# Transposing the middle values of an FFN by the DMA crossbar in two 16-bit planes

## The chip, the cores and the metric

The kernel runs on one core of one Trainium2 chip. The metric is device time in microseconds (us) of one execution.

## The reference

Two decoder layers run over one sequence of 512 positions with 1024 channels, all in float32. The first layer mixes with a recurrent block, the second with a chunked spatial gate. Around each mixer stand two feed-forward networks (FFN), four in all:

```python
def swiglu(x, w_in, w_out):
    g, u = jnp.split(x @ w_in, 2, axis=-1)
    return (jax.nn.silu(g) * u) @ w_out

for i in range(DEPTH):                       # DEPTH = 2
    h = h + 0.5 * swiglu(rms_norm(h, ffn1_norm[i]), ffn1_w_in[i], ffn1_w_out[i])
    hn = rms_norm(h, mix_norm[i])
    h = h + (recurrent_mixer(hn, ...) if i % 2 == 0 else spatial_gating_mixer(hn, ...))
    h = h + 0.5 * swiglu(rms_norm(h, ffn2_norm[i]), ffn2_w_in[i], ffn2_w_out[i])
return rms_norm(h, final_norm)
```

`w_in` is 1024 x 5632 and `w_out` 2816 x 1024. The middle values, `silu(g) * u`, are 512 x 2816.

## The kernel before

Every large product is computed with three float32r matmuls: each operand is split into a high part (`hi`, `whi`: a ScalarE copy with rounding) and the rest (`lo`, `wlo`: a VectorE subtraction), and hi x hi, lo x hi and hi x lo are added in PSUM (lines 385 to 387). On top of this, large blocks are multiplied by a scheme of seven products instead of eight (`seven`). Its left operands are sums of the four quarters A11, A12, A21, A22 of a block: S1 = A21 - A22 and, out of it, S2, S4 and S3 (`Group.s2`, `s4`, `s3`).

The unit of work is a step, a `Sub`: one weight tile of 128x1024 is loaded by the SP queue (line 135), for some products a second weight block is added by an accumulating DMA of the POOL queue (line 138) or by VectorE (line 87), the tile is split into `whi` and `wlo`, and the step's matmuls follow, mostly 12 of 128x512. All engines get their instructions in the order in which one loop over the steps writes them. In step i the loop splits the weights up to step i + 3 (`SPLIT_AHEAD`), runs what other code has hooked to the phases "pre", "mid" and "rest" of this step, asks for more weight loads, writes the step's matmuls, and runs "end" and "late". There are four buffers for `whi` and `wlo` and eight for raw weights. All other values lie in 60 slots of 128x512 float32 (`sp`).

An FFN is done in three parts (`FF_PARTS`): part 0 has a pair (2 column blocks of 128, `pair_plain`, eight steps) and a chunk of 4 column blocks (`chunk`, 14 steps), parts 1 and 2 have two chunks each. After the blocks of a part, `out_blocks` multiplies its middle values by the rows of `w_out`. In the first FFN, the pair's steps lie within the chunk of part 0.

The middle values come out with tokens on the partitions and are needed with channels on the partitions. `left_blocks` does that: it is called when the values of the first half of the tokens are ready (`half` 0: quarters A11 and A12) and again for the second half (A21 and A22). With `whole`, which the pair and the first chunk of parts 1 and 2 use, nothing is done for half 0, and after half 1 all quarters are transposed in one place: `Group.turn` writes TensorE transposes of 128x128 against an identity (line 267) into PSUM at a step's "end", 16 for a chunk and 8 for a pair. `Group.take` copies A11, A12 and A22 out of PSUM on ScalarE (line 96) and makes S1 from PSUM with one subtraction on VectorE (line 87). `Group.parts` then splits each left operand into hi and lo. The other chunks transpose each half by itself, and the steps below do not touch them.

Of the kernel before, what the change touches and what calls it, by code (L numbers as in the profile page):

```python
# [7 lines left out]

F32 = mybir.dt.float32
F32R = mybir.dt.float32r  # L10
AF = mybir.ActivationFunctionType
ALU = mybir.AluOpType

P = 128
D = 1024
T = 512
# [36 lines left out]
def trunk(ctx: ExitStack, tc: tile.TileContext, a: dict, out: bass.AP):  # L53
    nc = tc.nc
    PS = bass.MemoryType.PSUM
    cp = ctx.enter_context(tc.tile_pool(name="cp", bufs=1))
    sp = ctx.enter_context(tc.tile_pool(name="sp", bufs=SLOTS))
# [9 lines left out]
    def nm(s):  # L67
        uid[0] += 1
        return f"{s}_{uid[0]}"

    def slot(dt=F32, name="s"):
        return sp.tile([P, T], dt, tag="s", name=nm(name))
# [10 lines left out]
    def f32(t):  # L83
        return t.bitcast(F32)

    def tt(o, x, y, op):
        nc.vector.tensor_tensor(out=o, in0=x, in1=y, op=op)  # L87
# [4 lines left out]
    def stt(o, x, s, y, op0, op1):  # L92
        nc.vector.scalar_tensor_tensor(out=o, in0=x, scalar=s, in1=y, op0=op0, op1=op1)

    def act(o, x, f, **k):
        nc.scalar.activation(out=o, in_=x, func=f, **k)  # L96

    def split(src):

        w = src.shape[-1]  # L100
        hi, lo = slot(F32R, "hi")[:, :w], slot(F32R, "lo")[:, :w]
        act(hi, src, AF.Copy)
        tt(lo, src, f32(hi), ALU.subtract)
        return hi, lo
# [46 lines left out]
    class Sub:  # L151
# [19 lines left out]
        def split(self, between=None):  # L171

            if self.hi is not None:
# [4 lines left out]
            _, k, c = src.shape  # L178
            self.hi = wp.tile([P, 1024], F32R, tag="whi", name=nm("whi"))[:, : k * c].rearrange(
                "p (k c) -> p k c", k=k)  # L180
            self.lo = wp.tile([P, 1024], F32R, tag="wlo", name=nm("wlo"))[:, : k * c].rearrange(
                "p (k c) -> p k c", k=k)
            for q in ((slice(0, 1), slice(1, 2)) if self.raw.halves else (slice(0, k),)):
                act(self.hi[:, q, :], src[:, q, :], AF.Copy)
                tt(self.lo[:, q, :], src[:, q, :], f32(self.hi[:, q, :]), ALU.subtract)
# [29 lines left out]
    def hook(n, phase, fn):  # L215


        hooks.setdefault((n, phase), []).append(fn)
# [29 lines left out]
    class Group:  # L248
# [21 lines left out]
        def take(self, name, ps, gains=None):  # L270
# [11 lines left out]
            if gains is None:  # L282
                act(t, ps, AF.Copy)
            else:
                for q, g in zip(qs, gains):
                    act(t[:, q], ps[:, q], AF.Copy, scale=g)

        def direct(self, name, ps, gains):

            hi, lo = self.hl[name] = slot(F32R, "hi")[:, : self.n * H], slot(F32R, "lo")[:, : self.n * H]  # L290
            cs = [(slice(q * H, (q + 1) * H), g) for q, g in enumerate(gains)]
            for c, g in cs:
                act(hi[:, c], ps[:, c], AF.Copy, scale=g)
            for c, g in cs:
                stt(lo[:, c], ps[:, c], g, f32(hi[:, c]), ALU.mult, ALU.subtract)

        def stage(self, n, name, src, gains=None, parts=True, where=None, direct=0, turn=None, lag=0):


            st = {}  # L300
            hook(n if turn is None else turn, "end", lambda: st.update(ps=self.turn(src, where)))
            first = name == "A21"
            hook(n + 1, "pre" if first else "mid", lambda: self.take(name, st["ps"], gains))
            if direct:
                hook(n + direct, "mid", lambda: self.direct(name, st["ps"], gains))
            hook(n + max(direct, 1), "mid", st.clear)
            if parts:
                hook(n + 1 + lag, "mid", lambda: self.parts("S1" if first else name))
# [136 lines left out]
    def xt(t, n):  # L445
        return X[:, t, n * 512 : (n + 1) * 512]

    def square(t, n):
        junk = slot(name="junk")
        act(junk, xt(t, n), AF.Square, accum_out=ss[:, n * TT + t : n * TT + t + 1])  # L450

# [89 lines left out]
    class TileNorm:  # L541
# [29 lines left out]
        def take(self, half):  # L571
            for k in KORDER:
                ps = self.ps[k // 2][:, k % 2 * H : (k % 2 + 1) * H]
                if half == 0:
                    self.z[k] = (slot(F32R, "zh"), slot(F32R, "zl"))
                hi, lo = (t[:, half * H : (half + 1) * H] for t in self.z[k])
# [137 lines left out]
    def left_blocks(g, tiles, half, lag=1, whole=False, where=aux):  # L714


        def src(k, t0):
            return lambda q, s: tiles[t0 + s][:, (k * g.n + q) * P : (k * g.n + q + 1) * P]

        n = now[0] + lag  # L720
        if whole:
            if half == 0:
                return

            where = [bank, bank, None, None] if g.n == 2 else Halves(where).parts + Halves(aux).parts
            for at, name, k, t0, w in zip((n + 1, n + 2, n, n + 1), ("A11", "A12", "A22", "A21"), (0, 1, 1, 0), (0, 0, 2, 2),
                                          where):
                g.stage(at, name, src(k, t0), None, name != "A22", w, turn=n)
        elif half == 0:
            g.stage(n, "A11", src(0, 0))  # L730
            g.stage(n + 1, "A12", src(1, 0), turn=n)
            return
        else:
            g.stage(n, "A22", src(1, 2), None, False)
            g.stage(n + 1, "A21", src(0, 2), turn=n)
        sums(g, n + 3)
# [16 lines left out]
    def sums(g, n, s3=2):  # L753
        for i, fn in zip((0, 1, s3), (g.s2, g.s4, g.s3)):
            hook(n + i, "pre", fn)
# [12 lines left out]
    def chunk(w_in, f0, nt, group, opening=None, whole=False):  # L768
# [25 lines left out]
        def p3(s, ps):  # L794
            tt(c2[s], ps, c2[s], ALU.subtract)
            stt(c2[s], c2[s], rt(s), c1[s], ALU.mult, ALU.mult)
            ht[s] = c2[s]
            if s == 1:
                left_blocks(group, ht, 0, 2 if opening else 1, whole=whole)
# [5 lines left out]
        def q4(s, ps):  # L805
            s4 = slot(name="s4")[:, :w]
            act(s4, ps, AF.Silu, scale=rt(2 + s))
            stt(c5[s], c5[s], rt(2 + s), s4, ALU.mult, ALU.mult)
            ht[2 + s] = c5[s]
            if s == 1:  # L810
                left_blocks(group, ht, 1, whole=whole)
# [4 lines left out]
    def pair_plain(w_in, f0, group, first=False):  # L816
# [26 lines left out]
        def post(half):  # L843
            for s in range(2):
                ps, t = st[half, s], 2 * half + s
                if t not in ht:
                    silu(half, s)
                o = slot(name="h")[:, :w]
                stt(o, ps[:, w:], S.rt[:, t : t + 1], ht[t], ALU.mult, ALU.mult)
                ht[t] = o  # L850
            left_blocks(group, ht, half, 2, True, bank if first else aux)
# [52 lines left out]
    class FinalNorm:  # L904
# [86 lines left out]
        def keep(self, scale):  # L991
# [3 lines left out]
            def parts():  # L995
                self.x = split(xt(1, 1))
                self.eye = cp.tile([P, P], F32R, tag="eye", name="eye")
                act(self.eye, ident, AF.Copy, scale=1.0 / scale)
# [637 lines left out]
```

## Time and profile before

| | us |
|---|---|
| median of 3 runs | 1607.85 |
| range of the runs | 1607.69 to 1607.88 |
| span of the profiled execution, first to last instruction | 1607.4 |
| median less that span | 0.45 |
| TensorE matmul busy | 1598.5 (99%) |
| TensorE weight load busy | 1330.9 (83%) |
| VectorE busy | 1367.5 (85%) |
| ScalarE busy | 1037.4 (65%) |
| GpSimd busy | 222.6 (14%) |

All rows of the profile are from the one profiled execution. In a group's row stand the source line, engine, operation, written and read tiles, shape and count, then the busy time in us and the mean duration of one in ns, and the engine's idle time before it with what ended most of it. PE is TensorE's matmuls, PEld its weight loads, DVE VectorE, ACT ScalarE, POOL GpSimd, SPq the SP queue. In a row of the timeline stand start and duration in us; a bracket tells how long the engine had been idle and what released it.

### The profile page before, as it was taken

What the parts mean: (1) busy time and instruction counts of PE and PEld (TensorE: products, weight loads), DVE (VectorE), ACT (ScalarE), POOL (GpSimd) and SP (SyncE); (2) the same over time, 40 slices, a digit from 0 to 9 for tenths busy, and PEclk for the clock granted to TensorE, in tenths of its full rate; (3) what the DMA queues carried; (4) which work ended last, traced back from release to release, by engine and by line L of the source; (5) the groups of instructions that cost most, each with busy time, mean ns of one, the idle gap of its engine ahead of it and who ended that gap; (6) DMA issues with size and microseconds to landing.
All of it is one profiled execution on the core that took longest, in us unless ns stands there. A gap on an engine that the chain in (4) does not pass through costs nothing.

```text
span 1607.4 us, 20846 instructions
## 1 busy us (share of the span) xinstructions
PE 1598.5 (99%) x7453; PEld 1330.9 (83%) x7453; DVE 1367.5 (85%) x1834; ACT 1037.4 (65%) x1507; POOL 222.6 (14%) x201
## 2 busy tenths in 40 slices
PE   9999999999999999999999999999999999999998
PEld 7888888898888888888888888888888888888886
DVE  6998888888998787878987978878978988879778
ACT  7656556658777556656776565566886765565566
POOL 2111111100011111111101111111211011111110
PEclk9999999999999999999999999999999999999999
DMA  8877876944383786877837768768887557686793
GB/s 286 190 163 166 214 183 152 221 125 112 88 215 84 189 210 153 213 164 163 203 98 180 173 161 217 182 152 209 225 190 189 157 128 187 171 210 160 166 214 89
DMA packets 164264, 279.31 MB, mean 174 GB/s; under 512 B 11472, under 2 KB 37184, under 8 KB 164160
## 3 DMA queue, kind: packets, MB, share of 16 engines
q1 hardware_dynamic: 114656, 184.84, 36.7%
q0 software_dynamic: 47712, 91.30, 33.9%
q10 hardware_dynamic: 1792, 1.84, 0.4%
q8 instruction: 59, 0.97, 0.2%
q14 instruction: 45, 0.37, 0.1%
HBM read 275.84 MB, written 2.10 MB: 173 GB/s over the span
## 4 chain that ended last, share of the span: by engine, by line
PE 99%; DVE 0%; ACT 0%; issue 0%
PE A L386 14%; PE A L387 14%; PE A L385 14%; PE C L386 8%; PE C L387 8%; PE C L385 8%; PE p L834 5%; PE B L386 4%; PE B L385 4%; PE B L387 4%; PE e L267 4%; PE r L225 2%; PE r L226 2%; PE r L227 2%; PE Q L386 1%; PE Q L385 1%
## 5 line engine op out<-in xcount | busy, mean ns | idle before, releaser
L87 DVE TENSOR_TENSOR wlo<-raw,whi 128x1024 fp32r<-128x1024 f32 (+1 forms) x537 | 637.5, 1189 | 182.9 <-ACT whi L96 178.0
L96 ACT ACTIVATE whi<-raw 128x1024 fp32r<-128x1024 f32 (+1 forms) x537 | 554.9, 1034 | 368.5 <-PE A L386 116.4
L385 PE MATMUL A<-whi,hi 128*128 128x512 f32 x1016 | 399.3, 393 | 0.0
L387 PE MATMUL A<-wlo,hi 128*128 128x512 f32 x1016 | 395.9, 390 | 0.0
L386 PE MATMUL A<-whi,lo 128*128 128x512 f32 x1016 | 395.7, 389 | 0.0
L387 PEld LDWEIGHTS A<-wlo,hi 128*128 128x128 f32 x1016 | 190.7, 188 | 40.1 <-DVE wlo L87 0.4
L386 PEld LDWEIGHTS A<-whi,lo 128*128 128x128 f32 x1016 | 190.9, 188 | 38.4 <-DVE lo L87 0.3
L385 PEld LDWEIGHTS A<-whi,hi 128*128 128x128 f32 x1016 | 190.8, 188 | 38.2
L385 PE MATMUL C<-whi,hi 128*128 128x512 f32 x560 | 218.3, 390 | 0.0
L386 PE MATMUL C<-whi,lo 128*128 128x512 f32 x560 | 218.0, 389 | 0.0
L387 PE MATMUL C<-wlo,hi 128*128 128x512 f32 x560 | 218.0, 389 | 0.0
L138 POOL DMA_DIRECT2D raw<-in_ffn_w_in_dram x82 | 99.1, 1216 | 733.5 <-DVE raw L87 374.3
L138 POOL DMA_DIRECT2D raw<-in_ffn_w_out_dram x72 | 83.4, 1208 | 367.4 <-DVE wlo L87 181.9
L87 DVE TENSOR_TENSOR raw<-raw,raw 128x1024 f32<-128x1024 f32 x108 | 129.3, 1197 | 0.5
L96 ACT ACTIVATE hi<-a 128x512 fp32r<-128x512 f32 (+1 forms) x188 | 112.0, 601 | 19.1 <-DVE a L87 16.2
L87 DVE TENSOR_TENSOR lo<-a,hi 128x512 fp32r<-128x512 f32 (+1 forms) x188 | 122.0, 655 | 2.2 <-ACT hi L96 2.1
L386 PEld LDWEIGHTS C<-whi,lo 128*128 128x128 f32 x560 | 105.1, 188 | 22.4 <-DVE lo L87 0.7
L385 PEld LDWEIGHTS C<-whi,hi 128*128 128x128 f32 x560 | 105.1, 188 | 21.8
L387 PEld LDWEIGHTS C<-wlo,hi 128*128 128x128 f32 x560 | 105.1, 188 | 21.7
L96 ACT ACTIVATE c<-A 128x512 f32<-128x512 f32 x132 | 77.7, 597 | 70.3 <-PE A L387 70.3
L385 PE MATMUL B<-whi,hi 128*128 128x512 f32 x280 | 109.3, 390 | 0.0
L386 PE MATMUL B<-whi,lo 128*128 128x512 f32 x280 | 109.1, 389 | 0.0
(180 smaller groups left out, 2090.9 us busy)
## 6 DMA issues: line engine op xcount, KB each, us to landing
raw<-in_ffn_w_in_dram SPq DMA_DIRECT2D x161, 512.0 KB, 4.5
raw<-in_ffn_w_out_dram SPq DMA_DIRECT2D x100, 512.0 KB, 5.5
raw<-in_ffn_w_in_dram POOLq DMA_DIRECT2D x82, 512.0 KB, 7.0
raw<-in_ffn_w_out_dram POOLq DMA_DIRECT2D x60, 512.0 KB, 8.1
raw<-in_sg_w_in_dram SPq DMA_DIRECT2D x20, 512.0 KB, 7.0
raw<-in_ffn_w_in_dram SPq DMA_DIRECT2D x34, 256.0 KB, 5.1
raw<-in_rec_w_in_dram SPq DMA_DIRECT2D x16, 512.0 KB, 3.9
raw<-in_sg_w_in_dram POOLq DMA_DIRECT2D x12, 512.0 KB, 7.9
```

The lines of the kernel that those rows point to most:

```text
L87: nc.vector.tensor_tensor(out=o, in0=x, in1=y, op=op)
L96: nc.scalar.activation(out=o, in_=x, func=f, **k)
L138: nc.gpsimd.dma_start(out=self.v, in_=src, accum_op=ALU.add)
L225: nc.tensor.matmul(ps, wh, xh, start=start, stop=False)
L226: nc.tensor.matmul(ps, wh, xl, start=False, stop=False)
L227: nc.tensor.matmul(ps, wl, xh, start=False, stop=stop)
L267: nc.tensor.transpose(ps[:, o : o + P], src(q, s), ident)
L385: nc.tensor.matmul(ps, zh, wh, start=fresh and i == 0, stop=False, **k)
L386: nc.tensor.matmul(ps, zl, wh, start=False, stop=False, **k)
L387: nc.tensor.matmul(ps, zh, wl, start=False, stop=end, **k)
L834: nc.tensor.matmul(bank_of(half, s), z, (sub.lo if m == 2 else sub.hi)[:, q, :], start=left[2] == "2" and (h, q, m) == (0, 0, 0), stop=lef ...
```

## The change

For the pair and the first chunk of parts 1 and 2, `left_blocks` calls the new `Group.cross` for each half as it becomes ready, in place of TensorE's transposes. At "mid" of step n, ScalarE copies each of the half's two token tiles into two planes: the low and the high 16 bits of each float32, viewed as uint16 (`planes`). At "rest" of the same step, the SP queue issues four transposing DMAs from SBUF to SBUF, two for each of the half's two quarters (`move`). At "mid" of steps n + 3 and n + 4, ScalarE copies the transposed planes of one quarter each back into one float32 tile (`merge`). A21 is merged into the tile of S1, and VectorE subtracts A22 there at step n + 5 (`s1`). The hi and lo parts of A11, A12 and S1 are made from step n + 5 on, and S2, S4 and S3 follow at n + 6 to n + 8 of the second half. The planes and the transposed planes take slots of `sp`. The line numbers of the changed kernel are one larger at the helpers.

```diff
+        def cross(self, n, names, tiles):
+            w, pl, dt = 4 * self.n * P, [], {}
+            def planes():
+                for h in tiles:
+                    t = sp.tile([P, 2 * T], U16, tag="s", name=nm("pl"))[:, :w]
+                    act(t.rearrange("p (k b f) -> p k b f", k=2, b=2),
+                        h.bitcast(U16).rearrange("p (k f b) -> p k b f", k=2, b=2), AF.Copy)
+                    pl.append(t)
+                tiles.clear()
+            def move():
+                for name, k in names:
+                    d = dt[name] = sp.tile([P, 2 * T], U16, tag="s", name=nm("dt"))[:, :w]
+                    v = d.rearrange("p (m s t) -> p m s t", s=2, t=P)
+                    for s, t in enumerate(pl):
+                        nc.sync.dma_start_transpose(out=v[:, :, s, :], in_=t[:, k * w // 2 : (k + 1) * w // 2])
+                pl.clear()
+            def merge(name):
+                t = self.new("S1" if name == "A21" else name)
+                act(t.bitcast(U16).rearrange("p (x b) -> p b x", b=2), dt.pop(name).rearrange("p (b x) -> p b x", b=2), AF.Copy)
+            def s1():
+                tt(self.f["S1"], self.f["S1"], self.f["A22"], ALU.subtract)
+            hook(n, "mid", planes)
+            hook(n, "rest", move)
+            for i, (name, _) in enumerate(names):
+                hook(n + 3 + i, "mid", lambda name=name: merge(name))
+                if name in ("A11", "A12"):
+                    hook(n + 5 + i, "mid", lambda name=name: self.parts(name))
+            if names[-1][0] == "A21":
+                hook(n + 5, "pre", s1)
+                hook(n + 5, "mid", lambda: self.parts("S1"))
...
         n = now[0] + lag
         if whole:
-            if half == 0:
-                return
-
-            where = [bank, bank, None, None] if g.n == 2 else Halves(where).parts + Halves(aux).parts
-            for at, name, k, t0, w in zip((n + 1, n + 2, n, n + 1), ("A11", "A12", "A22", "A21"), (0, 1, 1, 0), (0, 0, 2, 2),
-                                          where):
-                g.stage(at, name, src(k, t0), None, name != "A22", w, turn=n)
-        elif half == 0:
+            g.cross(n, (("A22", 1), ("A21", 0)) if half else (("A11", 0), ("A12", 1)),
+                    [tiles.pop(2 * half + s) for s in range(2)])
+            if half:
+                sums(g, n + 6)
+            return
+        if half == 0:
```

More of the change, by code (lines that the diff above doesn't have):

```diff
@@ L10 @@
 F32R = mybir.dt.float32r
+U16 = mybir.dt.uint16
 AF = mybir.ActivationFunctionType
```

## The prediction

> **What bounds the kernel now.** I read the page first: busy time, then the chain that ended last, then the groups.
>
> ```profile
> span 1607.4 us, 20846 instructions
> PE 1598.5 (99%) x7453; PEld 1330.9 (83%) x7453; DVE 1367.5 (85%) x1834; ACT 1037.4 (65%) x1507; POOL 222.6 (14%) x201
> PE 99%; DVE 0%; ACT 0%; issue 0%
> L267 PE MATMUL e<-ident,c 128*128 128x128 f32 x352 | 44.4, 272 | 0.0
> L267 PE MATMUL e<-ident,h 128*128 128x128 f32 x32 | 4.1, 272 | 0.0
> ```
>
> TensorE is busy for 1598.5 of 1607.4 us and is 99% of the chain. So whatever TensorE no longer issues comes off the time, as long as its operands keep arriving. Line 267 is the transposes of the middle values. VectorE at 85% is the next engine; ScalarE has 35% free on average. The span is 0.45 us short of the median run, 1607.85; I put that 0.45 on top of every span below. A measurement of this kernel can tell about 0.2% (3.2 us) from no change.
>
> **Removed: 160 transposes on TensorE.** Each of the four FFNs has two first chunks (parts 1 and 2) of 16 transposes: 128 of the x352. The pair has 8 in each FFN: all x32 that read h. A duration of 272 ns overlaps its neighbours, so I take the price from the gap that a block makes in the weight loads.
>
> ```profile
> 259.22 0.19 PEld L387 LDWEIGHTS A<-wlo,hi 128*128 128x128 f32 x1
> 259.45 1.90 PEld L267 LDWEIGHTS e<-ident,c 128*128 128x128 f32 x16
> 261.31 0.19 PEld L385 LDWEIGHTS A<-whi,hi 128*128 128x128 f32 x1
> 261.43 0.19 PEld L386 LDWEIGHTS A<-whi,lo 128*128 128x128 f32 x1
> ...
> 508.15 0.19 PEld L387 LDWEIGHTS A<-wlo,hi 128*128 128x128 f32 x1
> 508.38 1.02 PEld L267 LDWEIGHTS e<-ident,h 128*128 128x128 f32 x8
> 509.37 0.19 PEld L385 LDWEIGHTS B<-whi,hi 128*128 128x128 f32 x1
> 509.48 0.19 PEld L386 LDWEIGHTS B<-whi,lo 128*128 128x128 f32 x1
> ```
>
> The loads come every 0.227 us (259.22 to 259.45). Without the block, the load now at 261.43 would stand at 259.45 + 0.23 = 259.68: the block costs 1.75 us, 0.109 per transpose. In the pair it is 509.48 - 508.61 = 0.87 us. Sum: 8 x 1.75 + 4 x 0.87 = 17.5 us. Nothing else hides these blocks, since TensorE does not wait around them.
>
> **Added on ScalarE.** Per chunk: four plane splits and four merges of 128x1024 16-bit elements; three copies out of PSUM go. No 16-bit operation is in this trace.
>
> ```profile
> L96 ACT ACTIVATE whi<-raw 128x1024 fp32r<-128x1024 f32 x507 | 536.2, 1058 | 362.7 <-PE A L386 113.6 <-DVE raw L87 79.1 <-PE C L386 71.0
> L96 ACT ACTIVATE a<-e 128x512 f32<-128x512 f32 x66 | 38.7, 586 | 2.6 <-PE e L267 2.6
> L96 ACT ACTIVATE a<-e 128x256 f32<-128x256 f32 x12 | 4.5, 371 | 0.0
> ```
>
> Bounds: by bytes a 128x1024 16-bit tile equals a 128x512 one, 0.59 us; by elements it is the whi row, 1.06; by the strided access it might be two passes, 2.1. I take 1.06, because count of elements is what the rows scale with (371, 586, 1058 ns for 256, 512, 1024). Per chunk: 8 x 1.06 - 3 x 0.59 = +6.7 us; per pair, at 512 elements, 8 x 0.59 - 3 x 0.37 = +3.6. In all 8 x 6.7 + 4 x 3.6 = 68 us: ScalarE goes from 1037 to about 1105 us, 70%. As an average that is free; the question is the place. ScalarE runs in order, and behind each added operation stand the whi splits that feed VectorE's wlo and then TensorE.
>
> The chunk at 220 to 260 us, steps of 12 matmuls (12 x 0.227 = 2.72 us):
>
> ```profile
> 248.76 1.06 ACT L96 ACTIVATE whi<-raw 128x1024 fp32r<-128x1024 f32 x1 [1.66 <-PE A L386]
> 250.35 0.60 ACT L96 ACTIVATE c<-A 128x512 f32<-128x512 f32 x1 [0.52 <-PE A L387]
> 251.71 0.60 ACT L96 ACTIVATE c<-A 128x512 f32<-128x512 f32 x1 [0.76 <-PE A L387]
> ...
> 254.21 1.07 ACT L96 ACTIVATE whi<-raw 128x1024 fp32r<-128x1024 f32 x1 [0.95 <-PE A L386]
> 255.79 0.69 ACT L96 ACTIVATE s<-A,rt 128x512 f32<-128x512 f32 x1 [0.52 <-PE A L387]
> 257.15 0.69 ACT L96 ACTIVATE s<-A,rt 128x512 f32<-128x512 f32 x1 [0.67 <-PE A L387]
> 257.74 1.05 ACT L96 ACTIVATE whi<-raw 128x1024 fp32r<-128x1024 f32 x1
> 259.88 1.06 ACT L96 ACTIVATE whi<-raw 128x1024 fp32r<-128x1024 f32 x1 [1.09 <-PE A L387]
> ...
> 247.67 0.75 DVE L93 SCALAR_TENSOR_TENSOR c<-c,rt,c 128x512 f32<-128x512 f32 x1
> ...
> 274.16 1.22 DVE L87 TENSOR_TENSOR wlo<-raw,whi 128x1024 fp32r<-128x1024 f32 x1
> ...
> 277.99 0.19 PEld L387 LDWEIGHTS A<-wlo,hi 128*128 128x128 f32 x1
> ```
>
> The brackets are ScalarE's idle time, each ended by TensorE giving back a buffer: ScalarE is ahead. First half: the two splits stand before the whi of 248.76, the second waits until VectorE has ended its c at 248.42, so they end near 249.4; that whi is 0.6 late and the idle before 250.35 and 251.71 takes it up. Merge A11 comes behind the whi of 254.21 (255.2 to 256.2), merge A12 and both splits of the second half behind that of 257.74, which moves to about 257.8: they end near 261.7, so the whi of 259.88 is 1.8 us late. Two merges follow one step apart. The lag peaks near 2 us. The shortest lead in this stretch is that of the wlo that ends at 275.38 (274.16 + 1.22) and is used at 278.21, when the matmul behind the load of 277.99 starts: 2.8 us. So 2 of 2.8 us is used up and TensorE does not stop.
>
> VectorE gets no more work: S1 was taken from PSUM with one subtraction and is now one subtraction in SBUF. But S1, S2, S4, S3 come three steps or so later, from its fullest stretch into a freer one:
>
> ```profile
> 40.00:55.00 15.00, 15.00 (x72) 12.50 (x71) 15.00 (x21) 10.60 (x17) 2.39 (x2) 1.00 0.74 125
> ...
> 250.00:260.00 10.00, 10.00 (x47) 8.27 (x46) 7.44 (x9) 5.66 (x8) 0.00 (x0) 1.00 0.53 166
> 260.00:270.00 10.00, 10.00 (x53) 8.55 (x52) 8.96 (x11) 7.71 (x12) 2.44 (x2) 1.00 0.81 153
> 270.00:280.00 10.00, 10.00 (x45) 8.28 (x45) 10.00 (x13) 8.09 (x12) 2.42 (x2) 1.00 0.63 91
> 280.00:290.00 10.00, 10.00 (x50) 8.35 (x49) 7.78 (x10) 5.58 (x7) 2.41 (x2) 1.00 0.94 288
> ```
>
> (Columns: PE, PEld, DVE, ACT, POOL busy, clock, DMA share, GB/s.) VectorE is 10.00 of 10 from 270, then 7.78. The products that read these parts come at least a chunk later. The one place without such room is the first FFN, where VectorE is busy 15.00 of 15 from 40 to 55; a pair's two splits there are 2 x 0.5 us of delay, of which I let 0.6 us through (bounds 0 and 1.1).
>
> **Added on the SP queue and the crossbar.** Per half chunk four transposing DMAs of 128 KB (pair: 64 KB), 96 in all, 10.5 MB. SP issues them in order, so the weight loads behind them wait for ScalarE's splits too. No transposing DMA is in this trace; the nearest rows are plain ones.
>
> ```profile
> raw<-in_ffn_w_in_dram SPq DMA_DIRECT2D x161, 512.0 KB, 4.5
> raw<-in_ffn_w_out_dram SPq DMA_DIRECT2D x100, 512.0 KB, 5.5
> raw<-in_ffn_w_in_dram SPq DMA_DIRECT2D x34, 256.0 KB, 5.1
> gw<-in_rec_gate_a_w_dram SPq DMA_DIRECT2D x4, 64.0 KB, 3.6
> ...
> 249.64 1.05 SPq L135 DMA_DIRECT2D raw<-in_ffn_w_in_dram  x2
> 256.88 27.00 SPq L135 DMA_DIRECT2D raw<-in_ffn_w_out_dram  x6
> ```
>
> Two issues take 1.05 us, and 512 KB lands 4.5 us after issue. If the four go like one 512 KB load, the last lands about 2 + 4.5 us after the first can start. Room: in the first half the first can start by 248.4, when the second split begins, and the second merge stands at 257.74 + 1.06 = 258.8: 10.4 us. In the second half the first split ends near 260.7; the second merge stands behind the whi three steps after that of 259.88, which is 259.88 + 8.16 - 1.75 (TensorE sooner) + 2 (lag) + 1.06 = 269.4: 8.7 us. It fits, so no merge waits. The other bound is one at a time at 5.1 us each, 20.4 us for four: the first rival. I take the near end, since the loads of these rows overlap in flight. For the weights: SP issues six in the 27 us from 256.88, so 5 us of transposes in front leave them time.
>
> The Trainium skill speaks on both sides. "VectorE: DVE Perf Modes", section "The three transpose paths", gives 1309 ns for a 128x128 16-bit block on the crossbar against 390 on TensorE, and its rules for authors say to use TensorE where a PSUM destination will do; an estimate by that price in a row, 16 blocks for a half, is 21 us, which would make the sum about 1591 + 8 x (9.5 + 7.8) = 1729. "Advanced Engine Details and Errata", section "X-Bar Transpose (TRN2)", says that transposing DMAs are as fast as regular ones, which goes with the forecast below. No row here shows either.
>
> **Sum.** 1607.4 - 17.5 + 0.6 = 1590.5, and 0.45 around it: 1591.0 us, 1.05% faster.
>
> **The rivals.**
>
> *The merges wait for the crossbar (slower).* ScalarE stands at a merge until its DMAs land, and the whi splits behind it stand too. It begins to cost when four transposes take longer than the room plus the 2.8 us lead: 11.5 us in the second half (2.9 us each), 13.2 in the first (3.3 each). At 5.1 us each, a chunk loses 20.4 - 11.5 = 8.9 and 20.4 - 13.2 = 7.2, together 16.1 us; pairs at 3.6 us (the 64 KB row), 14.4 against four steps of 2.72 and the lead, 13.7, lose 0.7 twice. 8 x 16.1 + 4 x 1.4 = 134: 1725 us. The time passes that of before at about 3.4 us each: 13.6 - 11.5 and 13.6 - 13.2 are 2.5 us per chunk, 20 in all. For it: 16-bit pieces are a use of the DMA engines that no row shows. Against: from 250 to 280 the DMA engines are busy for a share of 0.53 to 0.81, so there is room. Chance 0.21, anywhere from 1611 up.
>
> *ScalarE's 16-bit operations take two passes.* From 250 to 280 six of them at 2.1 us, less three copies, add 12.6 - 1.8 = 10.8 us to the 5.66 + 7.71 + 8.09 = 21.5 of the windows: 32.3 us of work in 30 - 1.75 = 28.25, less the lead of 2.8 a stall of 1.2 us per chunk, 1591 + 10 = 1601.
>
> For it: 16-bit elements with a stride of two. Against: ScalarE's rows follow the element count. Chance 0.11.
>
> *Transposes and weight loads share the DMA engines.* If each half takes 2.5 us of a load's time at a place where the lead is gone, 16 halves of chunks lose 1 us each: 1607. Against: the loads' leads. Chance 0.06.
>
> That the transposes stay is excluded: the changed program has 160 matmuls fewer, 60 ScalarE instructions and 96 DMAs more.
>
> **How the numbers follow.** Forecast 1591, chance 0.62, its own range 1588.5 (the 0.6 gone, splits by bytes) to 1597 (some merges late by half a microsecond). Faster: 0.62 + 0.11 = 0.73. Same: 0.06. Slower: 0.21. The range leaves out 0.03 below and most of the first rival: 1588.5 to 1620, which takes in its mild end.
>
> **What would show it.** Right: line 267 reading c x224 instead of x352, and no row that reads h; merges on ScalarE starting without a DMA as releaser; PE at 99% of a span near 1590; 16-bit ScalarE rows near 1060 ns. Wrong: ScalarE idle before the merges with the dt DMA as releaser and TensorE idle on wlo one to three steps on (first rival); 16-bit rows near 2.1 us (second); whi or POOL waiting for raw DMAs near the halves (third). The prediction falls if TensorE's idle time grows by more than 14 us.

## The result and the profile after

The changed kernel takes 1598.08 us (median of 4 runs, 1594.72 to 1601.47) against 1607.77 (1607.54 to 1607.88) for the kernel before in the same session: a ratio of 0.9940, 95% interval 0.9924 to 0.9955. It is faster by 9.7 us, where 16.9 were forecast. Its executions lie 6.7 us apart, those of before 0.3.

The profiled execution is the slowest of the four, 1601.47 us, with a span of 1599.8. In most executions with a recorded span, of this kernel and the others, the time is 1.65 to 1.8 us above the span. From the page of the changed kernel (busy times, the chain), and its groups with their shapes kept apart:

```profile
PE 1585.2 (99%) x7293; PEld 1314.5 (82%) x7293; DVE 1368.5 (86%) x1834; ACT 1098.4 (69%) x1567; POOL 223.1 (14%) x201
PE 90%; DMA 4%; DVE 3%; issue 1%; ACT 1%; SPq 0%; POOL 0%; ACTq 0%; DVEq 0%; POOLq 0%
...
L97 ACT ACTIVATE a<-dt 128x1024 uint16<-128x1024 uint16 x24 | 32.9, 1372 | 19.0 <-DMA dt<-pl 18.8
L97 ACT ACTIVATE pl<-c 128x1024 uint16<-128x1024 uint16 x32 | 32.9, 1054 | 2.7 <-DVE c L94 2.6
L268 PE MATMUL e<-ident,c 128*128 128x128 f32 x224 | 30.7, 274 | 4.0 <-DVE c L94 4.0
L97 ACT ACTIVATE a<-dt 128x512 uint16<-128x512 uint16 x12 | 9.3, 777 | 1.5 <-DMA dt<-pl 1.5
L97 ACT ACTIVATE pl<-h 128x512 uint16<-128x512 uint16 x16 | 9.0, 612 | 0.0
```

The transposes are gone (x224, and none reads h), and TensorE is still busy 99% of the span. But the chain is 90% TensorE where it was 99%: DMA and VectorE have entered it. ScalarE stands 18.8 us before its 128x1024 merges (`a<-dt`) for the transposing DMAs. The remaining transposes of c, with no idle time in their row before, stand 4.0 us for VectorE.

The transposed tiles alone (the view of one tile: the issues with their hold of SP in ns as smallest, median and largest, then who stood for them, then the time from issue to landing):

```profile
L315 SPq DMA_TRANSPOSE dt<-pl x96: 1182/1252/3072, 45.4 to 1523.3; - x96
...
  DMA dt<-pl: 24.6, 13
...
DMA to landing us min/median/max: 2.3/3.8/8.4
```

At the median each of the 96 holds SP for 1.25 us, where two plain issues took 1.05. It lands 2.3 to 8.4 us later, and in 13 places ScalarE stood, 24.6 us in all. The 18.8 us before the 128x1024 merges are those of the first merge in the second half of each of the eight chunks, 1.71 to 3.55 us each; in the first halves of the chunks no merge stood. The transfers differ by the half. One chunk as an example, first half and then second half: the landings, from the view of the tile in a window, and the row of the window (columns as in the prediction; the DMA share is the last but one):

```profile
DMA to landing us min/median/max: 2.3/2.4/2.5
605.00:612.00 7.00, 7.00 (x32) 5.79 (x32) 4.50 (x6) 4.91 (x7) 0.00 (x0) 1.00 0.52 125
...
DMA to landing us min/median/max: 6.2/7.5/8.2
618.00:630.00 12.00, 12.00 (x55) 9.94 (x54) 10.37 (x11) 8.08 (x10) 3.21 (x4) 1.00 1.07 157
```

In the first halves of the eight chunks a transfer landed 2.3 to 4.2 us after its issue, in the second halves 4.1 to 8.4. The slow landings go with the fuller DMA engines; no run changed that traffic alone.

To find where TensorE lost time I laid the matmuls that both kernels have against each other, in order, and looked where the offset jumps. (The offset is how much later a matmul starts in the changed kernel, each counted from the start of its span.) It falls by 1.67 us at each of the eight removed chunk blocks and by 0.80 at each pair: 16.6 us. It rises in two kinds of places. In the first FFN, between 55 and 90 us, it rises by 0.98, 1.65, 0.46, 0.88 and 1.45 us, and then by about 1.7 over some ten matmuls: 7.1 us. At the second chunk's own transposes of c, it rises by 0.71, 0.77, 1.65 and 0.42 (at 294, 645, 763 and 1545 us): 3.5 us. The three sums leave -6.0 us; at the last matmul the offset is -6.2.

The first FFN. The timeline of the changed kernel, SP, POOL, ScalarE and TensorE's weight loads, and then its windows (PE, PEld, DVE, ACT, POOL busy, clock, DMA share, GB/s):

```profile
59.03 5.04 SPq L315 DMA_TRANSPOSE dt<-pl  x4
64.19 6.67 SPq L136 DMA_DIRECT2D raw<-in_ffn_w_out_dram  x6
...
68.86 2.12 POOL L139 DMA_DIRECT2D raw<-in_ffn_w_out_dram  x2 [17.31 <-DVE wlo L88]
...
79.39 1.06 ACT L97 ACTIVATE whi<-raw 128x1024 fp32r<-128x1024 f32 x1 [4.14 <-DMA raw<-in_ffn_w_out_dram]
...
84.23 0.19 PEld L423 LDWEIGHTS C<-whi,hi 128*128 128x128 f32 x1 [1.14 <-ACT hi L97]
85.90 0.19 PEld L424 LDWEIGHTS C<-whi,lo 128*128 128x128 f32 x1 [1.49 <-DVE lo L88]
...
84.00:86.00 2.00, 0.59 (x2) 0.29 (x2) 2.00 (x5) 1.23 (x2) 0.00 (x0) 1.00 1.09 195
86.00:90.00 4.00, 4.00 (x11) 3.14 (x12) 4.00 (x7) 1.57 (x3) 1.20 (x1) 0.57 0.16 28
```

and of the kernel before at the same place:

```profile
52.03 16.19 SPq L135 DMA_DIRECT2D raw<-in_ffn_w_out_dram  x8
...
61.92 2.12 POOL L138 DMA_DIRECT2D raw<-in_ffn_w_out_dram  x2 [10.76 <-DMA raw<-in_ffn_w_out_dram]
```

Read it downwards. Four transposing DMAs hold SP from 59.03 to 64.07, and the six weight loads behind them are issued only from 64.19. POOL's two accumulating loads, which come on top, start at 68.86 where they started at 61.92. A weight split then stands 4.14 us for its load, and TensorE stops twice near 85 us. In the window after it the granted clock is 0.57, so that TensorE is busy for the whole 4 us and does 11 matmuls.

The second chunk, around 750 us. ScalarE and VectorE of the changed kernel, and TensorE's weight load of the transposes:

```profile
744.16 1.37 ACT L97 ACTIVATE a<-dt 128x1024 uint16<-128x1024 uint16 x1 [3.43 <-DMA dt<-pl]
747.74 1.36 ACT L97 ACTIVATE s<-dt 128x1024 uint16<-128x1024 uint16 x1 [1.31 <-DMA dt<-pl]
...
746.46 1.23 DVE L88 TENSOR_TENSOR wlo<-raw,whi 128x1024 fp32r<-128x1024 f32 x1 [1.68 <-ACT whi L97]
...
756.58 0.68 DVE L94 SCALAR_TENSOR_TENSOR s<-a,a 128x512 f32<-128x512 f32 x1
757.18 2.35 DVE L88 TENSOR_TENSOR wlo<-raw,whi 128x1024 fp32r<-128x1024 f32 x2
...
761.56 0.75 DVE L94 SCALAR_TENSOR_TENSOR c<-c,rt,c 128x512 f32<-128x512 f32 x1
...
762.37 0.75 PEld L268 LDWEIGHTS e<-ident,c 128*128 128x128 f32 x7 [1.19 <-DVE c L94]
```

and VectorE of the kernel before, the same sum S3 and the same c:

```profile
746.15 0.68 DVE L93 SCALAR_TENSOR_TENSOR s<-a,a 128x512 f32<-128x512 f32 x1
...
758.96 0.75 DVE L93 SCALAR_TENSOR_TENSOR c<-c,rt,c 128x512 f32<-128x512 f32 x1
```

ScalarE stands 3.43 and 1.31 us at the two merges, VectorE stands behind ScalarE (1.68 us ahead of the wlo at 746.46), and what it then has to catch up, the sums S2, S4 and S3 (the last is `s<-a,a`, 756.58) and the wlo, lies ahead of its own c: S3 starts 5.0 us ahead of the last c, where it was 12.8 us ahead in the kernel before. TensorE waits 1.19 us for that c.

### The profile page after: what moved, and what is told of

Read it like the earlier page. It is cut to its first block, busy times and chain, and to the rows that moved or that the text cites. A ratio compares the mean times of both kernels' runs of the same rounds, so it can differ in the third digit from the quotient of the medians.

```text
span 1599.8 us, 20767 instructions
## 1 busy us (share of the span) xinstructions
PE 1585.2 (99%) x7293; PEld 1314.5 (82%) x7293; DVE 1368.5 (86%) x1834; ACT 1098.4 (69%) x1567; POOL 223.1 (14%) x201
## 4 chain that ended last, share of the span: by engine, by line
PE 90%; DMA 4%; DVE 3%; issue 1%; ACT 1%; SPq 0%; POOL 0%; ACTq 0%; DVEq 0%; POOLq 0%
PE A L425 13%; PE A L424 13%; PE A L423 13%; PE C L424 7%; PE C L425 7%; PE C L423 7%; PE p L870 4%; PE B L425 4%; PE B L424 4%; PE B L423 4%; PE e L268 2%; PE r L226 2%; PE r L228 2%; PE r L227 2%; DMA raw<-in_ffn_w_in_dram 2%; DMA dt<-pl 1%
## 5 line engine op out<-in xcount | busy, mean ns | idle before, releaser
L97 ACT ACTIVATE hi<-a 128x512 fp32r<-128x512 f32 (+1 forms) x188 | 111.9, 600 | 18.8 <-DVE a L88 16.6
L425 PE MATMUL B<-wlo,hi 128*128 128x512 f32 x280 | 109.0, 389 | 0.0
```

The source lines that it names most:

```text
L425: nc.tensor.matmul(ps, zh, wl, start=False, stop=end, **k)
```

## The experiments

All times are medians in us. The kernel before stood at 1607.83 and 1607.77 in the first two sessions and at 1607.97 in the third; the changed kernel ran only in the session of its result.

**The first FFN taken out, or alone.** `left_blocks` gets an argument `old`, with which it takes the TensorE path of the kernel before. In first_pair_tensor only the first FFN's pair is old; in only_first_pair all else is.

```diff
-    def left_blocks(g, tiles, half, lag=1, whole=False, where=aux):
+    def left_blocks(g, tiles, half, lag=1, whole=False, where=aux, old=False):
...
+        if whole and old:
...
-            left_blocks(group, ht, half, 2, True, bank if first else aux)
+            left_blocks(group, ht, half, 2, True, bank if first else aux, first)
```

> The changed kernel, but the pair of the first FFN goes through TensorE as before; the other three pairs and all first chunks keep the crossbar. Theory A (most of the loss is local to the first FFN: a merge there waits for the crossbar, weight loads come late behind the transposing DMAs, TensorE stops and then runs at a lower granted clock): the 7.0 us that the trace shows lost between 55 and 90 us come back less 0.9 us of transposes, so 1592 to 1594 us, and the runs lie closer together than 1594.7 to 1601.5. Rival B (the loss is spread: every merge costs 1.37 us on ScalarE): 1597 to 1599 us.

> The kernel before, but the pair of the first FFN alone goes over the crossbar. Theory A: 0.9 us of transposes go and 7 us are lost, about 1614 us. Rival B: 1607 to 1608 us, no different from before.

first_pair_tensor took 1595.62 (1593.64 to 1601.65; ratio 0.9931, 0.9916 to 0.9946), 2.5 us less than the changed kernel, and the offset no longer rises between the start and 280 us. The time lies between theory A's and rival B's, the ranges of the two kernels overlap almost wholly, and two of its six executions stand at 1601 us: the executions did not come closer together. only_first_pair took 1609.87 (11 runs, 1609.00 to 1612.52; ratio 1.0014, 1.0005 to 1.0022), again between the two. So this one pair, which was to save 0.87 us, costs about 2 us. The 7.1 us above are what the slowest execution loses; in the profile of late_sums (below), an execution of 1598.27 us, the offset rises by 3.9 us in the same stretch. The timeline of only_first_pair, ScalarE, VectorE and TensorE's weight loads:

```profile
55.28 0.79 ACT L97 ACTIVATE a<-dt 128x512 uint16<-128x512 uint16 x1
55.92 1.13 ACT L97 ACTIVATE pl<-h 128x512 uint16<-128x512 uint16 x2
...
57.90 1.07 ACT L97 ACTIVATE whi<-raw 128x1024 fp32r<-128x1024 f32 x1
...
59.01 1.23 DVE L88 TENSOR_TENSOR wlo<-raw,whi 128x1024 fp32r<-128x1024 f32 x1 [1.98 <-ACT whi L97]
...
64.87 0.74 PEld L268 LDWEIGHTS e<-ident,c 128*128 128x128 f32 x7 [1.25 <-DVE c L94]
...
82.13 0.19 PEld L424 LDWEIGHTS C<-whi,lo 128*128 128x128 f32 x1 [1.31 <-DVE lo L88]
```

Here no merge waits for a DMA at all. A merge and two plane splits, 1.9 us, stand ahead of the whi of 57.90; VectorE idles 1.98 us for it in a stretch in which it had no room (14.81 of 15 us busy from 55 to 70 in the kernel before), its c comes late, and TensorE waits 1.25. A second stop, 1.31, comes at 82 us.

**The sums later.** In late_sums, S2, S4 and S3 of a first chunk come five steps later; both_cures has this and the old first pair.

```diff
-                sums(g, n + 6)
+                sums(g, n + (11 if g.n == 2 else 6))
```

> The changed kernel, but S2, S4 and S3 of a first chunk are computed at steps n + 11 to n + 13 of its second half, behind the next chunk's P3, in place of n + 6 to n + 8. Theory C (these sums, which the change moved later, stand on VectorE in front of the second chunk's c, and TensorE's remaining transposes wait for c: jumps of 0.7, 0.8, 1.65 and 0.4 us in the trace): 3.5 us come back, 1594.5 us. Rival D (c is late because ScalarE stood at the merges, whatever the sums do): less than 1 us, 1597.5 to 1599 us.

> First pair through TensorE and S2, S4, S3 later, the rest as changed. Theories A and C together: 17.5 - 0.9 us of transposes gone and nothing lost, 1590.5 to 1592 us, TensorE idle about 9 us as in the kernel before. If only A holds 1593 to 1595, if only C holds 1594 to 1597, if neither 1597 to 1599.

late_sums took 1598.27 (1594.28 to 1601.13; 0.9934, 0.9922 to 0.9946): no gain by itself, as rival D had it. both_cures took 1592.74 (1592.01 to 1596.91; 0.9912, 0.9897 to 0.9926), 2.9 us less than first_pair_tensor, though the ranges overlap; that is between what A alone and A with C were to give. In its trace one place is left at which the offset rises by over 0.25 us: 1.6 us at the second chunk near 287 us, in which the gate weights are split too. ScalarE still stood 22.4 us in 15 places before merges.

Theory C and rival D can be weighed by the traces, chunk by chunk: how long ScalarE stood before a chunk's merges, against the rise of the offset at that chunk's end (the chunk near 290 us left out). With the sums in their place, in the changed kernel and first_pair_tensor, up to 2.84 us of standing gave no rise over 0.25, 3.55 gave 0.41, 3.61 to 3.81 gave 0.72 to 0.77, and 4.74 gave 1.65. With the sums later, in late_sums and both_cures, up to 3.77 us gave no rise over 0.25, 3.89 gave 0.26, 4.22 gave 0.58, and 5.68 gave 1.74. So both have a part: it is the standing that costs, beyond about 3 us in a chunk, and the later sums let about 0.6 us more of it pass. late_sums had the longest standing of these profiles, 28.2 us in all. Near 290 us the rise does not follow the standing: it is 1.6 us in both_cures with 1.83 of it, and 2.0 in the next run with none.

**The merges later.** late_merge adds to both_cures that A22, A21 and S1 of a first chunk are merged two steps later.

```diff
-                hook(n + 3 + i, "mid", lambda name=name: merge(name))
+                hook(n + 3 + i + (2 if name in ('A22', 'A21') and self.n == 2 else 0), "mid", lambda name=name: merge(name))
...
-                hook(n + 5, "pre", s1)
+                hook(n + 5 + (2 if self.n == 2 else 0), "pre", s1)
```

> Built on both_cures (the first FFN's pair on TensorE, the sums S2, S4, S3 of a first chunk five steps later): the merges of a first chunk's second half (A22, A21) and S1 come two steps later too, so that the planes have more time to land. Theory A (what is left of the cost is ScalarE standing at merges whose transposing DMAs have not landed; in both_cures it stood 22.4 us in 15 places): ScalarE's idle time behind transposing DMAs falls below 8 us, the executions lie closer together, and the time is 1591.0 to 1591.8 us. Rival B (those stands cost TensorE nothing, since its weights are ready before it needs them): idle time falls as well, but the time stays at 1592.2 to 1593.2 us. Rival C (the later S1 is late for its products, or falls on VectorE's own c): 1594 us or more, with TensorE's weight load of c or of S1 waiting for VectorE.

It took 1592.92 (1592.08 to 1593.41; 0.9906, 0.9892 to 0.9920), as rival B said. The view of its transposed tiles:

```profile
  DMA dt<-pl: 1.5, 1
...
DMA to landing us min/median/max: 2.3/4.3/8.2
```

The transfers are as slow as before, and ScalarE's 22.4 us of standing are gone, yet the median is the same. No chunk of both_cures stood for more than 3.57 us, which TensorE bore with the sums out of the way. The highest run fell from 1596.91 to 1593.41, but with four and five runs that is no proof.

**The crossbar replaced by plain copies.** plain_copy leaves the transposition out: the same bytes go to the same tiles, but not transposed.

```diff
-  nc.sync.dma_start_transpose(out=v[:, :, s, :], in_=t[:, k * w // 2 : (k + 1) * w // 2])
+  nc.sync.dma_start(out=v[:, :, s, :], in_=t[:, k * w // 2 : (k + 1) * w // 2].rearrange("p (m t) -> p m t", t=P))
```

> The changed kernel with each of its 96 transposing DMAs replaced by a plain copy of the same 128 KB from the plane to the same tile; the transposition itself is left out. ScalarE's planes and merges, the steps and the removed TensorE work stay. Theory A (the crossbar's slowness, its long hold of SP and its late landing, costs the missing microseconds): a plain copy holds SP about 0.5 us and lands in 2.5 to 4 us, no merge stands, and the time is 1591 to 1593 us. Rival B (ScalarE's added 62 us and the moved steps cost it): 1596 to 1599 us, as the changed kernel. Rival C (copies between tiles in rows of 256 bytes are slower than the crossbar): 1600 us or more, with merges that stand longer than the changed kernel's 24.6 us.

1592.49 (1591.68 to 1592.92; 0.9903, 0.9887 to 0.9918). The view of its transposed tiles, and SP in the first FFN:

```profile
L315 SPq DMA_DIRECT2D dt<-pl x96: 593/612/1716, 44.8 to 1512.5; - x96
...
  DMA dt<-pl: 17.0, 16
...
DMA to landing us min/median/max: 1.9/3.6/9.0
...
56.91 2.63 SPq L315 DMA_DIRECT2D dt<-pl  x4
59.64 9.09 SPq L136 DMA_DIRECT2D raw<-in_ffn_w_out_dram  x6
```

The time is theory A's; its words on the merges are wrong, for they stand 17.0 us in 16 places. So in the steps of the changed kernel 5.6 of the missing 7.2 us come with the transposing DMAs, and the other 1.6 stay with plain copies. In this trace the offset still rises by 1.4 in the first FFN (0.91 and 0.48) and by 1.3 at two second chunks (0.86 and 0.45). The plain copy lands about as late as the transposing one (3.6 against 3.8 us), and late in the same places: 2.2 to 4.2 us in the chunks' first halves, 5.5 to 9.0 in the second, but for one copy. So the late landing is not the crossbar's. What clearly differs is the hold of SP, 0.61 against 1.25 us: four copies are through in 2.63 us, and the weight loads behind them start at 59.64, not 64.19.

**SP's order and ScalarE's order in the first FFN.** Three variants of only_first_pair: the pair's merges, parts, S1 and sums two steps later (ofp_late_merge), its transposing DMAs issued behind the step's weight loads (ofp_move_end), and both (ofp_late_end).

```diff
+            e = 2 if self.n == 1 else 0
...
-                hook(n + 3 + i, "mid", lambda name=name: merge(name))
+                hook(n + 3 + e + i, "mid", lambda name=name: merge(name))
...
-                sums(g, n + 6)
+                sums(g, n + 6 + (2 if g.n == 1 else 0))
```
```diff
-            hook(n, "rest", move)
+            hook(n, "end", move)
```

> Built on only_first_pair (1609.87 us, the kernel before with the first FFN's pair alone on the crossbar): that pair's merges, parts, S1 and sums come two steps later. Theory A (the loss in the first FFN comes from ScalarE's merges and planes standing before the steps' own weights, wherever they are put): 1609.3 to 1610.4 us, with TensorE's stops near 65 and 82 us again. Rival B (the loss comes from merges that stand before a weight's high part at those particular steps): 1607.0 to 1608.3 us. Rival C (it comes from the transposing DMAs on SP's queue ahead of the weight loads): no change, 1609.3 to 1610.4 us, and the stops come behind weights that landed late.

> Built on only_first_pair (1609.87 us): the transposing DMAs of that pair are issued at the end of the step, behind the weight loads of that step on SP's queue, in place of ahead of them. Theory A (ScalarE's order is what costs): no change, 1609.3 to 1610.4 us. Rival C (four transposing DMAs hold SP some 5 us and the weight loads behind them land late): 1607.0 to 1608.3 us, TensorE's stops near 65 and 82 us gone. Rival B (merges now wait for later transfers): 1611 us or more, with ScalarE idle behind transposing DMAs, which it was not in only_first_pair.

> Built on only_first_pair (1609.87 us) with both edits: the pair's merges, parts, S1 and sums two steps later (alone: 1609.62 us, the stop near 65 us gone, those near 82 us larger), and the transposing DMAs behind the step's weight loads (alone: 1608.67 us, the stop near 82 us gone, that near 65 us still there). Theory A (two separate causes, ScalarE's order at 65 us and SP's order at 82 us): both stops gone, the 0.87 us of the pair's removed transposes are seen, 1606.8 to 1607.3 us. Rival B (one crowded stretch: what is taken from one place comes back in the other): 1608.3 to 1609.8 us with a stop of over 1 us at 65 or 82 us.

| kernel | time | range (11 runs each) | ratio | rise of the offset near 65 and 75 us | near 82 us |
|---|---|---|---|---|---|
| only_first_pair | 1609.87 | 1609.00 to 1612.52 | 1.0014 (1.0005 to 1.0022) | 1.13, 0.47 | 1.05 |
| ofp_late_merge | 1609.62 | 1608.94 to 1611.58 | 1.0013 (1.0004 to 1.0022) | none | 1.08, 1.45 |
| ofp_move_end | 1608.67 | 1608.20 to 1612.49 | 1.0010 (1.0001 to 1.0019) | 1.17, 0.48 | none |
| ofp_late_end | 1607.71 | 1607.34 to 1608.19 | 0.9998 (0.9989 to 1.0007) | none | 0.24 |

Neither time decides by itself: 1609.62 lies in the ranges of theory A and rival C of its run, and 1608.67 between those of A and C. The traces do. Each edit takes away its own stop and leaves the other (in ofp_late_merge a larger one), and only both together end below every run of only_first_pair. So there were two causes: merges ahead of a whi on ScalarE, and transposing DMAs ahead of weight loads on SP. POOL shows the second, first in only_first_pair, then in ofp_late_end:

```profile
66.55 2.12 POOL L139 DMA_DIRECT2D raw<-in_ffn_w_out_dram  x2 [15.83 <-DMA raw<-in_ffn_w_out_dram]
```

```profile
61.48 1.20 POOL L139 DMA_DIRECT2D raw<-in_ffn_w_out_dram  x1 [10.14 <-DVE wlo L88]
```

The first accumulating load is back at 61.48, near the 61.92 of the kernel before (there two came at once; here the second follows at 68.98). The median missed its mark of 1606.8 to 1607.3 by 0.4 us: both stops are gone, but of the 0.87 us only 0.3 arrives against the kernel before, within the interval. In the trace the offset falls by 0.80 at 53 us and has crept back by 150 us, by 0.24 in one step near 80 us and in smaller ones; what holds TensorE there I did not find.

**The same order for all chunks.** move_after_loads is the changed kernel with that one "rest" made "end".

> The changed kernel with one edit: every transposing DMA is issued at the end of its step, behind that step's weight loads on SP's queue. Theory A (in the first FFN, the weight loads that stand behind four transposing DMAs of 1.25 us each land late, and that costs some 1.2 us in a typical execution, as between only_first_pair and ofp_move_end, and up to 4 us in a bad one): 1594.5 to 1597 us and fewer executions near 1601. Rival B (SP's order costs nothing that ScalarE's and VectorE's order does not cost as well): 1597.5 to 1599 us, as the changed kernel. Rival C (merges wait longer for the later transfers and the weights behind them are late): 1599.5 us or more, with ScalarE idle behind transposing DMAs for over 30 us (24.6 in the changed kernel).

1638.16 (1634.97 to 1647.10; 1.0185, 1.0171 to 1.0199): 30 us slower than before the change. Rival C named the way and the sign (74.6 us of standing), not the size. The stop near 82 us is gone in the trace, as theory A had it, and does not matter beside this. SP, ScalarE and TensorE at the second chunk, its window there, and the view of the transposed tiles:

```profile
261.99 6.39 SPq L136 DMA_DIRECT2D raw<-in_ffn_w_out_dram  x2
268.49 8.71 SPq L315 DMA_TRANSPOSE dt<-pl  x4
...
282.30 1.34 ACT L97 ACTIVATE a<-dt 128x1024 uint16<-128x1024 uint16 x1 [8.03 <-DMA dt<-pl]
283.52 1.03 ACT L97 ACTIVATE whi<-raw 128x1024 fp32r<-128x1024 f32 x1
...
284.60 0.79 PE L423 MATMUL A<-whi,hi 128*128 128x512 f32 x1 [3.34 <-ACT whi L97]
...
280.00:290.00 10.00, 6.48 (x20) 4.17 (x19) 3.99 (x5) 7.70 (x11) 1.20 (x1) 0.83 0.85 108
...
  DMA dt<-pl: 74.6, 15
```

Here is the first rival of the prediction at work: a merge stands 8.03 us, the whi behind it stands too, and TensorE stops 3.34 us for that whi. The transposing DMAs start at 268.49, behind weight loads that hold the queue for 6.39 us. In the changed kernel the same four start at 266.26, with the chunk at the same place (the first matmul behind the removed block starts at 264.9 us there, at 264.8 here), they land 5.8 to 6.7 us after their issue where they land 7.2 to 13.2 here, and the merge stands 1.75 us. A part of the loss is the clock: the window's granted clock is 0.83, and in this profile, of the slowest execution, six stretches behind such stops, 23.8 us together, have a granted clock of 0.50 to 0.51. TensorE is busy for 21.85 of them, so by an estimate at half the clock some 11 us are lost in matmuls that run slower. The changed kernel has one such stretch, at 86 us.

**All of it.** all_late has the whole change, the first pair too, with late_merge's and ofp_late_end's times.

```diff
+            e = 2 if self.n == 1 or names[0][0] == "A22" else 0
...
-            hook(n, "rest", move)
+            hook(n, "end" if self.n == 1 else "rest", move)
...
-                hook(n + 3 + i, "mid", lambda name=name: merge(name))
+                hook(n + 3 + e + i, "mid", lambda name=name: merge(name))
...
-                sums(g, n + 6)
+                sums(g, n + (11 if g.n == 2 else 8))
```

> All of the change, the first FFN's pair too, with the times moved: second-half merges and S1 of a first chunk two steps later and its sums five steps later (as in late_merge), the pair's merges, parts, S1 and sums two steps later and its transposing DMAs behind the step's weight loads (as in ofp_late_end). Theory A (both causes in the first FFN are gone): 1592.0 us, 0.9 below late_merge's 1592.92. Rival B (the first FFN has no room for the pair's planes and merges wherever they stand): 1593.5 to 1595 us.

The chain in its profile, with a span of 1590.3 us:

```profile
PE 98%; DVE 1%; ACT 1%; DMA 0%; issue 0%; SPq 0%; DVEq 0%
```

1592.16 (1591.93 to 1592.68; 0.9902, 0.9889 to 0.9916), as theory A had it: 15.8 us below the kernel before, and 5.9 below the changed kernel. It has the lowest median of all versions, though the ranges of both_cures and late_merge overlap it. The chain is TensorE's again, merges stand 0.5 us in one place, and the only rise of the offset over 0.25 us is 0.98 at the second chunk with the gate weights. It does the changed kernel's work with the same DMAs; only the steps differ.

## Why the prediction was right or wrong, point by point

**The number: the forecast missed, the wide range held.** 1598.08 lies above the forecast's own range, 1588.5 to 1597. The range to 1620 holds it because it takes in the mild end of the first rival, and it was that mechanism which came. The 0.45 us between span and time was of one execution, and most others show 1.65 to 1.8; nothing hangs on it, since the sum is the median before less 16.9 us.

**The sign and the bound: right.** TensorE is the bound, and what it no longer issues comes off the time. all_late brought 15.8 of the 16.9 us.

**160 transposes, 17.5 us: right, a little large.** The offset falls by 8 x 1.67 + 4 x 0.80 = 16.6 us. The gap between two weight loads overstated a block by 0.07 to 0.08 us.

**ScalarE's price: right for the sum, wrong for a part.** The splits took 1054 ns (forecast 1060), the merges 1372; ScalarE's busy time rose by 61.0 us (forecast 68). Two passes, the second rival, are out. The pair's, forecast at 0.5 to 0.59, took 0.61 and 0.78.

**"TensorE does not stop", since the lag of 2 us is under the lead of 2.8: wrong for the step, since it counted work and no standing.** ScalarE stood 1.75 and 3.43 us at merges on top of it. The lead itself was about right: up to 2.84 us of standing in a chunk gave no rise of the offset over 0.25.

**"It fits, so no merge waits": wrong, and this is the step that failed.** The term that was mis-sized is the landing of the last of the four, 6.5 us after the first can start. At 266 us in the changed kernel:

```profile
266.26 6.94 SPq L315 DMA_TRANSPOSE dt<-pl  x4
...
274.31 1.38 ACT L97 ACTIVATE a<-dt 128x1024 uint16<-128x1024 uint16 x1 [1.75 <-DMA dt<-pl]
```

The issues alone hold SP for 6.94 us, where 2 us were put for them, and each transfer lands 5.8 to 6.7 us after its own issue, where 4.5 were put. So the last landed 10.5 us after the first issue, in a room put at 8.7. And the room was worked out for a half's second merge alone. What stood was the first merge, one step of 2.72 us earlier, so with some 6 us of room by the same working: two of the four transfers suffice for it, and it could start 8.05 us after the first issue. "So there is room", from a DMA share of 0.53 to 0.81, did not hold: from 266 to 277 us the share is 0.97 in the changed kernel. The price of the first rival, one transfer at a time, was wrong on the other side: they do overlap, for the fourth was issued at 270.9 us and its merge started at 277.00 without waiting, 10.7 us after the first issue where four in a row were put at 20.4. The mild form came true, with a few microseconds, and move_after_loads shows the steep part of that rival: in that order, with transposing DMAs that start 2.2 us later in the chunk shown, the kernel is 40 us slower.

**"VectorE gets no more work" and the sums move "into a freer" stretch: right on the work (1368.5 us against 1367.5), wrong on the place.** VectorE's free time there went into standing behind ScalarE, and the sums then stood ahead of c. Putting them later brought 2.9 us beside first_pair_tensor, none beside the changed kernel; by the chunks it lets about 0.6 us more of standing pass.

**The first FFN, 0.6 us let through (bounds 0 and 1.1): mis-sized.** By only_first_pair the loss is 2.0 + 0.87 = 2.9 us, and it is 7.1 in the profiled execution of the changed kernel. The bounds held only the two splits. They left out the merges, and that SP's weight loads, and POOL's accumulating loads after them, move back behind four transposing DMAs. The sentence that "5 us of transposes in front leave them time" was read from a chunk at 257 us and didn't hold for the first FFN. The sign named for the third rival, whi and POOL waiting for raw loads, is seen there, but by the order of the queue: ofp_late_end has the same transfers and no stop over 0.25 us. What the sharing of the DMA engines may have slowed is the transposing DMAs themselves, in the chunks' second halves (1.07 against 0.52 of share); this is argued, not shown.

**The pages.** The Trainium skill's "VectorE: DVE Perf Modes", section "The three transpose paths", gives 1309 ns for one 128x128 block on the crossbar, by which the estimate was 1729 us. Here 1252 ns is the hold of SP by one DMA, and 64 of the 96 carry four blocks each, so the trace does not bear out a price per block in a row. The Trainium skill's "Advanced Engine Details and Errata", section "X-Bar Transpose (TRN2)", has transposing DMAs as fast as regular ones. plain_copy agrees for the landing (3.6 against 3.8 us) and not for the issue (0.61 against 1.25 us).

**What stays open.** Why executions of the changed kernel lie 6.7 us apart. late_merge and all_late, in which merges hardly wait, lie within 1.4 us, but so do the plain copies, whose merges wait, and only_first_pair, in whose profile no merge waits, lies 3.5 us apart; I only argue that landing times that differ between executions meet deadlines without slack. Why c is late near 290 us in every version that changes that chunk, with and without standing. And plain_copy shows that the transposing DMAs cost 5.6 us, and the first FFN that SP's order is a part of it, but no run changed SP's hold alone.

## What to carry to other kernels

When work leaves the bound engine for a DMA, price the issue on its queue and what is queued behind it, including loads of another queue that come on top, and not only the landing. A step that is moved "into freer time" has to be checked in the order of the engine's instructions: free time there may be standing behind the very engine that gets the new work. Here the last third of the gain came from steps alone: consumers of the slow transfer two steps later, their successors five, and the first FFN's transfers behind the weight loads. Issuing the transfers later was ruinous for the chunks, so each place in a queue has to be tried by itself. And ask which consumer of a batch comes first: here the room was worked out for the last.

## What the runs showed of the hardware

A transposing DMA from SBUF to SBUF, 128 or 64 KB, held SP for 1.25 us at the median, up to 3.07, where a plain copy of the same size held it 0.61. Both landed within about 2 to 9 us: 2.2 to 4.2 in the chunks' first halves, mostly 5.5 to 9 in the second, at a DMA share of 0.52 and 1.07 in the chunk looked at. A ScalarE copy of 1024 16-bit elements took 1054 ns when the source is strided and 1372 when the destination is. After TensorE stood for 1.4 of 2.0 us (84 to 86 us), the profile shows a granted clock of 0.57 over the next 4 us (86 to 90 us), and the matmuls in them took about 1.7 us longer than the same ones of the kernel before.
